# Pooling's window sums as scans on VectorE, and v's weight splits queued earlier, in a transformer-like layer on one core

## The chip, the cores and the metric

The kernel runs on one core of one Trainium2 chip. The metric is the device time of one execution in microseconds (us), as the median of several runs. The engines are named PE (TensorE, matrix products), DVE (VectorE), ACT (ScalarE), POOL (GpSimd) and SP (SyncE, which here only issues DMAs).

## The reference

One layer over 512 tokens of width 1024, all in float32. Cut to what matters here:

```python
POOL_WINDOWS = (2, 4, 8, 16)
def pool_mixer(u, w_pool, pool_scale):
    for g, w in enumerate(POOL_WINDOWS):
        ug = u32[..., g * POOL_GROUP:(g + 1) * POOL_GROUP]
        cs = jnp.cumsum(ug, axis=1)
        cs_lag = jnp.pad(cs, ((0, 0), (w, 0), (0, 0)))[:, :S]
        mean = (cs - cs_lag) / jnp.minimum(pos, float(w))
        outs.append(mean - ug)
    p = jnp.stack(outs, axis=2)
    y = jnp.einsum('bsgi,gij->bsgj', p, w_pool)
    return y.reshape(u.shape) * pool_scale

def reference(x, ...):
    h = rms_norm(x, norm_mix)
    u_pool, u_lru, q, k, v, g_logits = jnp.split(h @ w_in, splits, axis=-1)
    gates = jax.nn.sigmoid(g_logits + b_gate)
    y_pool = pool_mixer(u_pool, w_pool, pool_scale)
    y_lru = rglru_mixer(u_lru, ...)                 # convolution, gates, recurrence over tokens
    y_sb = stick_breaking_attention(rms_norm(q), rms_norm(k), v)
    merged = sum(gates[i] * (y_i @ w_branch[i]))    # three branches
    x = x + merged @ w_out
    h2 = rms_norm(x, norm_ffn)
    return x + (silu(h2 @ w_ffn_gate) * (h2 @ w_ffn_up)) @ w_ffn_down
```

The pooling mixer takes, for each of 4 groups of 256 channels, the mean over the last 2, 4, 8 or 16 tokens, less the token itself.

## The kernel before, in words

Channels lie on the 128 partitions and tokens along the free dimension, so one row of pooling is a tile of 128 channels by 512 tokens; a group `g` has two rows `j`, and a row's names carry both (`p20h` is group 2, row 0). Every product is made of three matmuls (`mm3`, lines 304 to 306): each operand is split into a high part, which ACT copies out, and a low part, which DVE computes as the difference. For a weight tile this is `split_w` (lines 139 and 140, tiles `whi` and `wlo`), for a pooling row `split_hl` (lines 932 and 933, `p20h` and `p20l`), for the attention's weights `wth` and `wtl` (lines 1105 and 1106), for queries and keys `qkh` and `qkl` (lines 1056 and 1057). The next matmuls wait for both.

The order of each engine's instructions is set by a scheduler that goes through the program in the order in which it is written, but takes work of a higher priority sooner: `with tc.high_priority(n)` moves what stands in it ahead by about n places. Weight tiles are made by `emit_next`, three at a time ahead of their use, with a priority of `AHEAD` = 200. Each has one of three buffers, which PE frees.

The program runs in stages. First come the input norm, the gates and the input projection of the recurrence (up to about 139 us). Then v, k and q are projected, each as seven products of half-size blocks by Strassen's scheme: the products are named 11, 12, S2, S1, S3, S4, 22 in this order (v is `t` = 2, its weight splits have keys `("seven", 2, ...)`, and the matmuls stand in line 828). While v is projected, DVE also finishes the recurrence: `lru_input` (704, 705) and `lru_scan` (711, a scan on DVE). S2 adds to the sum in PSUM that ACT copies out of 11 (`snap`, line 841), and S3 to that of S2.

From about 289 us on, the four chunks of pooling are projected (`ps_pool`), in the order 1, 0, 3, 2 of the groups, and then the branch projections (`ps_br`). Between them, from a list of background tasks (`tick`), the attention's heads and the pooling's own steps are put in: ACT copies the row out of PSUM (`evac_u`, line 975, tile `up`); `pool_mean` takes the sums of 2, 4, 8 or 16 tokens by doubling, in one, two, three or four steps of one short copy and one addition each (lines 983 and 984, tiles `pw`), corrects the first columns (987), forms mean less token (989) and splits the result; `pool_back` multiplies with the group's weights (`pps`). In the attention, scores `z` go through two sigmoids (`K`, `A`), a scan on DVE (line 1090, `E`), and a product (1092), are turned on PE (`pw` of line 1103), copied and split (`wth`, `wtl`), and multiplied with v (`py`). The turned tiles, `pq`, `pps` and `py` share three PSUM buffers, so `pq` of one head has to wait until the `wtl` of another has read its tile.

After that come the third branch, the output projection and the feed-forward part, in which nothing changes.

Of the kernel before, what the change touches and what calls it, by code (L numbers as in the profile page):

```python
# [12 lines left out]
ALU = mybir.AluOpType  # L13
# [4 lines left out]
S = 512  # L18
# [15 lines left out]
AHEAD = 200  # L34
# [30 lines left out]
def layer_kernel(ctx: ExitStack, tc: tile.TileContext, x, xt, vecs, w_in, w_qkv7, w_gate7, w_pool, w_rg, w_ig,  # L65
# [3 lines left out]
    dve = nc.vector  # L69
# [216 lines left out]
    def emit_next():  # L286
        i = state["i"]
        if i >= len(specs):
            return
        state["i"] = i + 1  # L290
        key, make = specs[i]
        with tc.high_priority(AHEAD if i > 6 else 0):
            ready[key] = make(str(i))

    def weights(*key):
        while key not in ready:
            emit_next()
        while len(ready) < 3 and state["i"] < state["stop"]:
            emit_next()
        return ready.pop(key)  # L300
# [134 lines left out]
    with ExitStack() as first:  # L435
# [39 lines left out]
        for k in range(2):  # L475
# [4 lines left out]
            make_h(k)  # L480
        load_xt(2)
        emit_next()
        make_h(2)
        load_xt(3)
# [435 lines left out]
    def slot(name, dt=F32, shape=(S,)):  # L920
        return sp.tile([P] + list(shape), dt, tag="s", name=name, bufs=NSP - NLD)
# [7 lines left out]
    def split_hl(src, nm):  # L929
        h = slot_r(nm + "h")  # L930
        l = slot_r(nm + "l")
        act(h, src, AF.Copy)
        dve.tensor_tensor(l, src, h.bitcast(F32), ALU.subtract)
        return h, l

    with ExitStack() as mix:
# [14 lines left out]
        ahead = ap1.tile([P, S], BF16, tag="ahead", name="ahead")  # L951
# [25 lines left out]

        def pool_mean(g, j, u):
            w = 2 << g
            prev, sh = u, 1  # L980
            while sh < w:
                nxt = slot(f"pw{g}{j}{sh}")
                dve.tensor_copy(nxt[:, 0:sh], prev[:, 0:sh])
                dve.tensor_tensor(nxt[:, sh:], prev[:, sh:], prev[:, 0:S - sh], ALU.add)
                prev = nxt
                sh *= 2
            dve.scalar_tensor_tensor(prev[:, 0:w - 1], prev[:, 0:w - 1], float(w),
                                     invpos[:, 0:w - 1], ALU.mult, ALU.mult)
            dve.scalar_tensor_tensor(u, prev, 1.0 / w, u, ALU.mult, ALU.subtract)
            pool_p.setdefault(g, []).append(split_hl(u, f"p{g}{j}"))  # L990
# [21 lines left out]
        def pool_chunk(g):  # L1012
            pss = chan_chunk(("pool", g), hn, 1)
            us = [evac_u(pss[j], f"up{g}{j}", g == POOL[3]) for j in range(2)]
            for j in range(2):
                bg.append(lambda j=j, u=us[j]: pool_mean(g, j, u))
            if g != POOL[0]:
                queue_pool_back(POOL[POOL.index(g) - 1])
# [713 lines left out]
```

## Time and profile before

| | us |
|---|---|
| median of 3 runs | 871.65 (871.23 to 871.83) |
| profiled execution, its own time | 871.86 |
| its span in the trace | 870.1 |
| PE busy | 860.3 |
| DVE busy | 740.7 |
| ACT busy | 522.7 |

The granted clock of PE is full throughout. Busy times are sums over all stages; what an engine costs is seen only in the stretch in which another engine waits for it. In the rows of a timeline the columns are start and duration in us, engine, line, operation, the tile written, the tiles read, and in brackets how long the engine had been idle and what ended that. In a row of who waited for whom they are the waiting engine, its tile and line, what it waited for, and then the total in us, the number of times and the longest.

### The profile page before, as it was taken

The numbers are of one execution on the slowest core, as the hardware profiler recorded it, in microseconds if no ns is written. First come the engines' busy times: TensorE is split into PE (matmuls) and PEld (weight loads), VectorE is DVE, ScalarE is ACT, GpSimd is POOL, SyncE is SP. The second block draws the span as 40 slices with busy tenths as digits, with TensorE's granted clock in tenths as the row PEclk, the third lists the DMA queues.
The fourth block names the chain that finished last, engine by engine and source line by source line (L and its number), as shares of the span: only waits on it lengthen the run. The fifth ranks groups of instructions, "written<-read, shape, count | busy, mean of one in ns | idle before, by whom it ended". The sixth has DMA issues, their size and how long they took to land.

```text
span 870.1 us, 14264 instructions
## 1 busy us (share of the span) xinstructions
PE 860.3 (99%) x5563; PEld 790.2 (91%) x5563; DVE 740.7 (85%) x961; ACT 522.7 (60%) x727; POOL 91.1 (10%) x130
## 2 busy tenths in 40 slices
PE   9999999999999999999999999999999999999998
PEld 7888878888899988889889998889999999999998
DVE  7899897998796598977988796699998888899974
ACT  6554989556966566465664545454555555755642
POOL 1110002232433101000001200000000000121200
PEclk9999999999999999999999999999999999999999
DMA  9586346799592776644636955346543333798913
GB/s 338 164 288 205 98 166 184 212 328 253 174 306 73 236 224 207 217 121 148 212 102 169 197 179 170 97 132 160 147 120 97 108 112 113 230 244 202 191 41 121
DMA packets 116643, 154.08 MB, mean 177 GB/s; under 512 B 8160, under 2 KB 90080, under 8 KB 116576
## 3 DMA queue, kind: packets, MB, share of 16 engines
q1 hardware_dynamic: 103904, 107.30, 38.3%
q0 software_dynamic: 12528, 45.62, 22.0%
q8 instruction: 43, 0.70, 0.3%
q10 hardware_dynamic: 144, 0.26, 0.1%
q14 instruction: 24, 0.20, 0.1%
HBM read 132.71 MB, written 18.87 MB: 174 GB/s over the span
## 4 chain that ended last, share of the span: by engine, by line
PE 84%; DVE 8%; ACT 5%; issue 1%; DMA 1%; SPq 0%; DVEq 0%; ACTq 0%
PE ps_y L313 11%; PE ps_x L313 8%; PE ps_q L828 7%; PE ps_dy L1651 6%; PE ps_dx L1651 5%; PE ps_gate L731 3%; PE ps_bY L1276 2%; PE ps_gy L313 2%; PE ps_br L305 2%; PE ps_br L304 2%; PE ps_br L306 2%; DVE wlo L140 2%; PE ps_bX L1276 2%; PE ps_gx L313 2%; PE ps_lru L304 1%
## 5 line engine op out<-in xcount | busy, mean ns | idle before, releaser
L139 ACT ACTIVATE whi<-raw 128x1024 fp32r<-128x1024 f32 x69 | 72.9, 1056 | 76.1 <-PE ps_out L305 16.0
L140 DVE TENSOR_TENSOR wlo<-raw,whi 128x1024 fp32r<-128x1024 f32 x69 | 84.4, 1224 | 24.7 <-ACT whi L139 24.1
L140 DVE TENSOR_TENSOR wlo<-qw,whi 128x1024 fp32r<-128x1024 f32 x48 | 58.5, 1221 | 16.4 <-ACT whi L139 16.3
L139 ACT ACTIVATE whi<-qw 128x1024 fp32r<-128x1024 f32 x48 | 50.6, 1054 | 28.8 <-PE ps_q L828 14.8
L1437 ACT ACTIVATE wh_S<-w_S 128x1024 fp32r<-128x1024 f32 x36 | 38.3, 1063 | 30.3 <-PE ps_y L313 18.3
L1557 POOL DMA_DIRECT2D dw<-in_w_down_dram x20 | 16.9, 847 | 305.4 <-DMA dw<-in_w_down_dram 261.8
L1438 DVE TENSOR_TENSOR wl_S<-w_S,wh_S 128x1024 fp32r<-128x1024 f32 x36 | 43.9, 1223 | 3.3 <-ACT wh_S L1437 3.3
L1437 ACT ACTIVATE wh<-w 128x1024 fp32r<-128x1024 f32 x27 | 28.6, 1060 | 27.8 <-PE ps_x L313 9.1
L1438 DVE TENSOR_TENSOR wl<-w,wh 128x1024 fp32r<-128x1024 f32 x27 | 33.0, 1223 | 8.2 <-ACT wh L1437 8.2
L1437 ACT ACTIVATE whdS<-dw 128x1024 fp32r<-128x1024 f32 x20 | 21.2, 1060 | 21.6 <-PE ps_dy L1651 10.6
L1438 DVE TENSOR_TENSOR wldS<-dw,whdS 128x1024 fp32r<-128x1024 f32 x20 | 24.3, 1223 | 5.5 <-ACT whdS L1437 5.5
L1090 DVE TENSOR_TENSOR_SCAN E<-K,ahead 128x512 f32<-128x512 f32 (+3 forms) x32 | 25.4, 814 | 4.0 <-ACT K L1086 4.0
L304 PE MATMUL ps_lru<-HH,whi 128*128 128x512 f32 x64 | 24.6, 384 | 0.0
L304 PE MATMUL ps_br<-yph,whi 128*128 128x512 f32 x64 | 24.5, 383 | 0.0
L304 PE MATMUL ps_pool<-HH,whi 128*128 128x512 f32 x64 | 24.5, 383 | 0.0
L304 PE MATMUL ps_br<-yHH,whi 128*128 128x512 f32 x64 | 24.5, 383 | 0.0
L304 PE MATMUL ps_gate<-HH,whi 128*128 128x512 f32 x64 | 24.4, 381 | 0.0
L305 PE MATMUL ps_lru<-HL,whi 128*128 128x512 f32 x64 | 24.3, 379 | 0.0
L306 PE MATMUL ps_lru<-HH,wlo 128*128 128x512 f32 x64 | 24.3, 379 | 0.0
L305 PE MATMUL ps_gate<-HL,whi 128*128 128x512 f32 x64 | 24.3, 379 | 0.0
L306 PE MATMUL ps_gate<-HH,wlo 128*128 128x512 f32 x64 | 24.3, 379 | 0.0
L305 PE MATMUL ps_pool<-HL,whi 128*128 128x512 f32 x64 | 24.3, 379 | 0.0
(740 smaller groups left out, 3445.7 us busy)
## 6 DMA issues: line engine op xcount, KB each, us to landing
raw<-in_w_in_dram SPq DMA_DIRECT2D x31, 512.0 KB, 5.1
qw<-in_w_qkv_dram SPq DMA_DIRECT2D x24, 512.0 KB, 7.1
dw<-in_w_down_dram POOLq DMA_DIRECT2D x20, 512.0 KB, 8.0
w<-in_w_ffn_gate_dram SPq DMA_DIRECT2D x36, 256.0 KB, 3.8
w<-in_w_ffn_up_dram SPq DMA_DIRECT2D x36, 256.0 KB, 4.2
raw<-in_w_branch_dram SPq DMA_DIRECT2D x16, 512.0 KB, 3.6
qw<-in_w_qkv_dram POOLq DMA_DIRECT2D x12, 512.0 KB, 8.0
qd<-r POOLq DMA_DIRECT2D x12, 512.0 KB, 7.3
```

Source lines behind the costliest of these rows:

```text
L139: act(hi, raw, AF.Copy)
L140: dve.tensor_tensor(lo, raw, hi.bitcast(F32), ALU.subtract)
L304: nc.tensor.matmul(ps, lh, rh, start=start, stop=False, skip_group_check=skip)
L305: nc.tensor.matmul(ps, lh, rl, start=False, stop=False, skip_group_check=skip)
L306: nc.tensor.matmul(ps, ll, rh, start=False, stop=stop, skip_group_check=skip)
L313: nc.tensor.matmul(o, a_[a][:, w, k, :], il2(b_[b][:, k, :]), start=first and n == k == 0, stop=last and n == 2 and k == 3, skip_group_che ...
L731: nc.tensor.matmul(pss[n // 2][n % 2], w[:, k % 2, n * P:(n + 1) * P], il(hu[k][x_]), start=k == 0 and w is wh and x_ == 0, stop=k == KT - ...
L828: nc.tensor.matmul(ps[:, a, :], b_[:, k, ts_], il(a_[:, kk, :]), start=first and n == k == 0, stop=n == 2 and k == 3, skip_group_check=True)
L1276: nc.tensor.matmul(o, ah[x_][:, w, k, :], il2(b[k][y_]), start=first_ and n == k == 0, stop=n == 2 and k == 3, skip_group_check=True)
L1437: act(h, src, AF.Copy)
L1438: dve.tensor_tensor(l, src, h.bitcast(F32), ALU.subtract)
L1651: nc.tensor.matmul(o, a_[a][:, w, k0 + k, :], il2(b_[b][:, k, :]), start=first and i == k == 0, stop=last and i == 2 and k == nk - 1, skip ...
```

## The change

Two edits. In `pool_mean` the sum of windows 4, 8 and 16 is made by two scans along the row instead of doublings: the first runs over the first w columns (running sum from 0, with the zeros of the tile `ahead` as second operand), the second over the other 512 - w, adding the new token and subtracting the one that leaves the window, and starting from the first's last column. The window of 2 keeps its copy and addition. In `emit_next` the splits of v's weights get the priority 320 instead of 200.

```diff
-        with tc.high_priority(AHEAD if i > 6 else 0):
+        with tc.high_priority((320 if key[:2] == ("seven", 2) else AHEAD) if i > 6 else 0):
             ready[key] = make(str(i))
...
         def pool_mean(g, j, u):
             w = 2 << g
-            prev, sh = u, 1
-            while sh < w:
-                nxt = slot(f"pw{g}{j}{sh}")
-                dve.tensor_copy(nxt[:, 0:sh], prev[:, 0:sh])
-                dve.tensor_tensor(nxt[:, sh:], prev[:, sh:], prev[:, 0:S - sh], ALU.add)
-                prev = nxt
-                sh *= 2
+            prev = slot(f"pw{g}{j}")
+            if w == 2:
+                dve.tensor_copy(prev[:, 0:1], u[:, 0:1])
+                dve.tensor_tensor(prev[:, 1:], u[:, 1:], u[:, 0:S - 1], ALU.add)
+            else:
+                dve.tensor_tensor_scan(prev[:, 0:w], u[:, 0:w], ahead[:, 0:w], 0.0, ALU.add, ALU.add)
+                dve.tensor_tensor_scan(prev[:, w:], u[:, w:], u[:, 0:S - w], prev[:, w - 1:w], ALU.add, ALU.subtract)
             dve.scalar_tensor_tensor(prev[:, 0:w - 1], prev[:, 0:w - 1], float(w),
                                      invpos[:, 0:w - 1], ALU.mult, ALU.mult)
             dve.scalar_tensor_tensor(u, prev, 1.0 / w, u, ALU.mult, ALU.subtract)
```

On DVE, while v is projected, the order of the splits against the recurrence: `wlo_1395` is of product S2, `wlo_1470` and `wlo_1486` are the first and second split of S3, line 711 is the recurrence's scan.

```order
 L140 TENSOR_TENSOR wlo_1368<-qw_1206,whi_1367 128x1024
 L207 TENSOR_TENSOR qw_1204<-qw_1204,qs_1262 128x1024
+L140 TENSOR_TENSOR wlo_1395<-qs_1262,whi_1394 128x1024
 L207 TENSOR_TENSOR qw_1206<-qw_1206,qs_1302 128x1024
-L140 TENSOR_TENSOR wlo_1395<-qs_1262,whi_1394 128x1024
 L140 TENSOR_TENSOR wlo_1411<-qs_1302,whi_1410 128x1024
```

```order
+L140 TENSOR_TENSOR wlo_1470<-qw_1200,whi_1469 128x1024
 L711 SCALAR_TENSOR_TENSOR li_898<-lt_1118,ls_1249 128x512 x2
-L140 TENSOR_TENSOR wlo_1470<-qw_1200,whi_1469 128x1024
 L711 SCALAR_TENSOR_TENSOR li_1083<-lt_1224,ls_1251 128x512
 L140 TENSOR_TENSOR wlo_1486<-qw_1202,whi_1485 128x1024
```

The first split of S2 passes one addition, the first of S3 passes two scans; the second split of S3 has the same rows ahead of it as before. On ACT, the copies for these splits pass the copy of line 841 that stood ahead of them.

On DVE in the pooling, the sums of the row p20 (numbers of buffers differ between the kernels); a scan is listed as SCALAR_TENSOR_TENSOR with `ahead` or the tile itself as second source. Before:

```order
L983 COPY pw_3444<-up_3347 128x1
L984 TENSOR_TENSOR pw_3444<-up_3347 128x511
L983 COPY pw_3447<-pw_3444 128x2
L984 TENSOR_TENSOR pw_3447<-pw_3444 128x510
L983 COPY pw_3450<-pw_3447 128x4
L984 TENSOR_TENSOR pw_3450<-pw_3447 128x508
L140 TENSOR_TENSOR wlo_3462<-raw_3459,whi_3461 128x1024
L1106 TENSOR_TENSOR wtl_2735<-pw_0_3409,wth_2732 128x512
```

After:

```order
L985 SCALAR_TENSOR_TENSOR pw_3420<-up_3323,ahead 128x8
L986 SCALAR_TENSOR_TENSOR pw_3420<-up_3323,pw_3420 128x504
L987 SCALAR_TENSOR_TENSOR pw_3420<-pw_3420,invpos 128x7
L989 SCALAR_TENSOR_TENSOR up_3323<-pw_3420,up_3323 128x512
L933 TENSOR_TENSOR p20l<-up_3323,p20h 128x512
L140 TENSOR_TENSOR wlo_3432<-raw_3429,whi_3431 128x1024
L1106 TENSOR_TENSOR wtl_2735<-pw_0_3385,wth_2732 128x512
```

Six instructions became two, and the whole rest of the row (987, 989, 933), which stood behind the `wtl` of the attention, now stands ahead of it. On ACT at the same place, before:

```order
L139 ACTIVATE whi_3461<-raw_3459 128x1024
L1105 ACTIVATE wth_2732<-pw_0_3409 128x512
L1105 ACTIVATE wth_2733<-pw_1_3416 128x384
L1105 ACTIVATE wth_2734<-pw_2_3422 128x384
L1086 ACTIVATE K_2741<-z_1_3428,qrs 128x128
```

After:

```order
L932 ACTIVATE p20h<-up_3323 128x512
L139 ACTIVATE whi_3431<-raw_3429 128x1024
L1105 ACTIVATE wth_2732<-pw_0_3385 128x512
L1105 ACTIVATE wth_2733<-pw_1_3392 128x384
L1105 ACTIVATE wth_2734<-pw_2_3398 128x384
```

`p20h`, which waits for DVE's line 989, now stands ahead of `whi` and `wth`; it stood behind them. The row p30 moved in the same way.

## The prediction

> **What bounds the kernel now.** I read the profile's page first, then who made the matrix engine (PE) wait, then the busy time by stretch, then the timelines of PE and the vector engine (DVE) at the places found.
>
> ```profile
> span 870.1 us, 14264 instructions
> PE 860.3 (99%) x5563; PEld 790.2 (91%) x5563; DVE 740.7 (85%) x961; ACT 522.7 (60%) x727; POOL 91.1 (10%) x130
> ```
>
> PE is busy for all but 9.8 us, and the change leaves every matmul where it was. So it can only win back time in which PE stands still, and only where DVE or ACT holds it. The waits of PE, and DVE's load by stretch (columns: window, span, then busy time and count of PE, PEld, DVE, ACT, POOL):
>
> ```profile
> PE pq L1053 <- DVE wtl L1106: 1.7, 2, 1.5
> PE ps_q L828 <- DVE wlo L140: 1.2, 3, 0.7
> PE pps L304 <- DVE qkl L1057: 0.2, 1, 0.2
> ```
>
> ```profile
> 139.00:171.00 32.00, 30.84 (x141) 26.06 (x140) 30.66 (x27) 22.78 (x25) 6.54 (x8) 1.00 0.63 169
> 299.00:350.00 51.00, 51.00 (x266) 45.37 (x265) 46.42 (x84) 32.73 (x58) 4.28 (x8) 1.00 0.76 231
> 350.00:360.00 10.00, 8.49 (x51) 7.38 (x50) 9.93 (x21) 4.09 (x9) 0.00 (x0) 1.00 0.82 273
> 375.00:400.00 25.00, 25.00 (x141) 22.26 (x140) 18.70 (x28) 13.56 (x26) 0.00 (x0) 1.00 0.51 154
> ```
>
> DVE is full at 139 to 171 (v's products beside the recurrence) and at 350 to 360 (pooling beside attention); PE loses 1.2 and 1.5 us there. After 375 DVE has a quarter free, and PE does not wait. Each half of the change touches one of the two. The orders of PE, of the DMA queue of SP and of GpSimd stay as they were, word for word, so no transfer passes another; only DVE and ACT are reordered. The pooling wait in PE's own rows:
>
> ```profile
> 354.62 0.38 PE L306 MATMUL ps_br<-yHH,wlo 128*128 128x512 f32 x1
> 356.51 1.12 PE L1053 MATMUL pq<-idn,at 128*128 128x128 f32 x8 [1.51 <-DVE wtl L1106]
> ...
> 362.09 0.28 PE L306 MATMUL z<-qkh,qkl 128*128 128x256 f32 x1
> 362.54 0.48 PE L304 MATMUL pps<-p30h,wph 128*128 128x512 f32 x1 [0.17 <-DVE qkl L1057]
> 362.86 0.38 PE L305 MATMUL pps<-p30l,wph 128*128 128x512 f32 x1
> ```
>
> Ends of matmuls are modelled, so I count start to start. A 512-column product follows the last after 0.22 us. From 354.62 PE could have gone on at 354.84 but went on at 356.51: 1.67 lost. A 256-column product passes in half that, 0.11: from 362.09 PE could have gone on at 362.20, so 0.34 is lost, and the next step is 0.32 instead of 0.22: 0.10 more, together 0.44. The pooling stretch can give back 1.67 + 0.44 = 2.1 us, whatever DVE saves beyond that.
>
> **The pooling sums.** The new operation is a scan, and the trace has scans of other operands on DVE (busy, mean ns of one):
>
> ```profile
> L989 DVE SCALAR_TENSOR_TENSOR up<-pw,up 128x512 f32<-128x512 f32 x8 | 5.5, 688 | 0.1
> L984 DVE TENSOR_TENSOR pw<-up 128x511 f32<-128x511 f32 x8 | 5.5, 682 | 0.0
> L1090 DVE TENSOR_TENSOR_SCAN E<-K,ahead 128x512 f32<-128x512 f32 x4 | 4.9, 1217 | 0.0
> L1090 DVE TENSOR_TENSOR_SCAN E<-K,ahead 128x128 f32<-128x128 f32 x3 | 1.3, 418 | 0.0
> L987 DVE SCALAR_TENSOR_TENSOR pw<-pw,invpos 128x7 f32<-128x7 f32 x2 | 0.3, 156 | 0.0
> ```
>
> (1217 - 418) / 384 = 2.08 ns a column: a scan of 496 to 508 columns takes 1.18 to 1.21 us, one of 4 to 16 columns 0.16 to 0.19. No row shows a scan of an addition and a subtraction, nor one whose start value is a tensor's column. I take the row's price; from below the bound is a plain addition (0.68), from above twice the row (2.4). [...] At the lower bound the sum below would change by no more than 0.15 us, since PE itself is then the limit.
>
> What the doublings took, and the path to the 1.67 us (DVE):
>
> ```profile
> 328.76 0.14 DVE L983 COPY pw<-up 128x1 f32<-128x1 f32 x1
> 331.80 1.61 DVE L1106 TENSOR_TENSOR wtl<-pw,wth 128x512 fp32r<-128x512 f32 x3
> ...
> 347.01 1.22 DVE L140 TENSOR_TENSOR wlo<-raw,whi 128x1024 fp32r<-128x1024 f32 x1 [0.74 <-ACT whi L139]
> 348.15 0.74 DVE L1003 SCALAR_TENSOR_TENSOR ypl<-pps,vt,yph 128x512 fp32r<-128x512 f32 x1
> 348.81 1.21 DVE L1090 TENSOR_TENSOR_SCAN E<-K,ahead 128x512 f32<-128x512 f32 x1
> ...
> 352.39 0.15 DVE L983 COPY pw<-up 128x1 f32<-128x1 f32 x1
> 354.64 1.22 DVE L140 TENSOR_TENSOR wlo<-raw,whi 128x1024 fp32r<-128x1024 f32 x1
> 355.77 1.62 DVE L1106 TENSOR_TENSOR wtl<-pw,wth 128x512 fp32r<-128x512 f32 x3
> ...
> 361.13 0.69 DVE L933 TENSOR_TENSOR p20l<-up,p20h 128x512 fp32r<-128x512 f32 x1 [0.70 <-ACT p20h L932]
> ```
>
> Four doublings (window 16) took 331.80 - 328.76 = 3.04 us, three (window 8) 354.64 - 352.39 = 2.25: 0.75 a doubling. The two scans take about 0.2 + 1.1 = 1.3 from start to start (an instruction's successor starts some 0.1 before its end: 347.01 to 348.15 for 1.22). So a row of 16 saves 1.7, one of 8 saves 0.95, one of 4 saves 2 x 0.75 - 1.3 = 0.2. Two rows of each: 5.7 us of DVE. Of that, 2 x 0.2 + 2 x 1.7 + 0.95 = 4.8 us lies ahead of 355.77.
>
> PE does not get 4.8, for the order moved as well. The sum's end (`up`) goes to ACT for `p..h` and back for `p..l`; for p11 and p30 the weight split that used to fill that trip now stands behind it, and the price of an empty trip is the 0.70 in the last row above. And on ACT `p20h` now stands ahead of the split and of `wth`, which `wtl` needs. So I walk the path from its last tie to PE: the weight split (`whi`) whose buffer PE frees after this product, and on ACT in the old order
>
> ```profile
> 342.99 0.38 PE L306 MATMUL ps_pool<-HH,wlo 128*128 128x512 f32 x1
> ...
> 350.32 1.06 ACT L139 ACTIVATE whi<-raw 128x1024 fp32r<-128x1024 f32 x1
> 351.28 1.34 ACT L1105 ACTIVATE wth<-pw 128x512 fp32r<-128x512 f32 x3
> ```
>
> In the new order I place that `whi` at 343.45 (one `yph` stands ahead of it on ACT), so its `wlo` on DVE at 344.5, not 347.01. From `wlo` to the pooling of window 8 it took 352.39 - 347.01 = 5.38; one `ypl` (348.81 - 348.15 = 0.66) has moved ahead of it: 4.72, so 349.2. The scans 1.3, the first columns 0.2, the closing product 0.7: 351.4. ACT's `p20h` sends DVE on at 352.1; ACT's `whi` then takes 351.28 - 350.32 = 0.96 and is done at 353.05; DVE's `wlo` 1.13: `wtl` starts at 354.25 instead of 355.77. PE's `pq` started 356.51 - 355.77 = 0.74 after `wtl`: 354.99, against 354.84 at which PE is ready. So 1.52 of the 1.67 comes back. The second wait is for `qkl`, which stood behind the closing product and split of p20; now it follows `wtl` after the three `wtl` (1.5), two scans (1.2), and two passes of 0.6: it starts at 357.55 and is done by 358.3, while PE wants it at 362.20 - 1.52 = 360.7. So the 0.44 goes, with 2 us of cover. Pooling: 1.52 + 0.44 = 1.96 us; bounds 0.9 (one more trip to ACT left open on the path and nothing at the second wait) and 2.1.
>
> **The splits of v's weights.** One DVE order change matters: the first split for S3 passes two scans of the recurrence. DVE, then PE:
>
> ```profile
> 159.05 2.33 DVE L711 TENSOR_TENSOR_SCAN li<-lt,ls 128x512 f32<-128x512 f32 x2
> 161.30 1.20 DVE L140 TENSOR_TENSOR wlo<-qw,whi 128x1024 fp32r<-128x1024 f32 x1
> 162.42 1.22 DVE L711 TENSOR_TENSOR_SCAN li<-lt,ls 128x512 f32<-128x512 f32 x1
> 163.55 1.20 DVE L140 TENSOR_TENSOR wlo<-qw,whi 128x1024 fp32r<-128x1024 f32 x1
> ```
>
> ```profile
> 162.55 0.48 PE L828 MATMUL ps_q<-wlo,hT3h 128*128 128x512 f32 x1 [0.68 <-DVE wlo L140]
> 162.87 0.38 PE L828 MATMUL ps_q<-whi,hT3l 128*128 128x512 f32 x1
> ...
> 165.25 0.38 PE L828 MATMUL ps_q<-wlo,hT3h 128*128 128x512 f32 x1
> ...
> 167.62 0.38 PE L828 MATMUL ps_q2S<-whi,HH 128*128 128x512 f32 x1
> ```
>
> Moved to 159.05, that split ends at 160.25 and PE's wait of 0.68 goes. What is late next is S3's second split: before it stand the same DVE instructions, so it still starts at 163.55 and ends at 163.55 + 1.20 = 164.75. Before, PE came to it at 165.25; now PE is there first and goes on at 164.80, with 0.32 for the first step and ten of 0.216: S4 starts at 167.28 instead of 167.62, a gain of 0.34. The wait that the S2 split removes only brings PE to that same split sooner. On ACT a split passes the copy `r` three times (1.0 us each); PE needs that copy only a product later, so it costs nothing, but 0.3 if it should be late. Bounds: 0 and 1.2 (all three waits).
>
> **Sum.** 1.96 + 0.34 = 2.3 us off the profiled execution's 871.86: 869.56. The median is 0.21 below that execution: **869.4 us**.
>
> **The rivals.** *ACT's order eats the pooling gain.* `p30h` and `p20h` now make ACT wait for DVE ahead of `wth`, `K` and `whi`; one more exposed trip (0.70) and one `whi` (0.96) behind it leave 2.3 - 1.6 = 0.7 us, about 870.9. For it: DVE has 46.42 of 51 us filled before 350 and the path is tight to 0.15 us; against it: 4.8 us saved. [...]
>
> *v gives nothing* because S3's second split falls back by the 0.45 us that it had to spare (164.80 to 165.25): 869.7, still faster.
>
> *Lost again later*: PE, two microseconds sooner, waits for loads that do not come sooner. DMA is 0.51 busy after 375, so I give it little; about 871.
>
> *Slower*: the new scan costs much more than the row. Three large scans lie on the path between 328 and 355; with x more each and nothing hidden, `wtl` comes 3x later. The gains of 1.52 and 0.34 and a 0.2% loss of 1.74 are used up at 3x = 3.6, so from x = 1.2, a scan at twice the row. At 3.0 us (x = 1.8) the time is 871.65 + 5.4 - 1.86 = 875.2. Nothing in the trace speaks for it but that no row shows this form. That the change doesn't do what it says I exclude: the order shows both scans and the moved splits.
>
> **Chances.** Forecast 0.54, v nothing 0.10 (both faster); ACT's order 0.20 and lost later 0.07 (both within); slower 0.09. A measurement tells about 0.2%, 1.74 us, so faster means below 869.9: 0.64; within 0.27; slower 0.09. The range runs from 868.4 (2.1 and 1.2 us together) to 871.2, past the two cases within; it leaves out the slow scan and the edges.
>
> **What would show it.** Right: large scans of about 1.2 us; PE's wait for `wtl` near 355 under 0.3 us and for `qkl` near 360 gone; one wait of PE for the second S3 split near 164, S4 about 0.3 us earlier; no new wait near 334. Wrong: scans over 2 us, PE held by `wtl` at 334, or the gain gone by 460.

## The result, and the profile after

| | us |
|---|---|
| median before, 22 runs beside those of the change | 871.62 (870.99 to 872.79) |
| median after, 22 runs | 870.28 (869.95 to 871.04) |
| ratio, 95% interval | 0.9986 (0.998 to 0.9992) |
| profiled execution of after, its own time | 870.05 |
| its span | 868.3 |

The change is faster by 1.3 us. That is inside the forecast range, 0.9 us above the forecast, and at 0.14% it lies within the 0.2%, for which I had given 0.27. The head of the page of after (engine, busy us, share of the span, instructions), then who made PE wait:

```profile
span 868.3 us, 14234 instructions
PE 859.3 (99%) x5563; PEld 789.9 (91%) x5563; DVE 736.4 (85%) x937; ACT 522.3 (60%) x727; POOL 91.0 (10%) x130
```

```profile
PE ps_q L828 <- DVE wlo L140: 1.1, 2, 0.8
PE pq L1053 <- DVE wtl L1106: 1.0, 3, 0.7
```

The row of `pps` that waited for `qkl` is gone, but `pq` still waits 1.0 us for `wtl`, in three places instead of two. PE's timeline after, at four places (`...` marks rows left out, here and below):

```profile
164.04 0.48 PE L828 MATMUL ps_q<-wlo,hT3h 128*128 128x512 f32 x1 [0.84 <-DVE wlo L140]
...
332.38 0.38 PE L306 MATMUL ps_pool<-HH,wlo 128*128 128x512 f32 x1
332.94 0.80 PE L1053 MATMUL pq<-idn,at 128*128 128x128 f32 x5 [0.18 <-DVE wtl L1106]
...
354.23 0.38 PE L306 MATMUL ps_br<-yHH,wlo 128*128 128x512 f32 x1
355.26 0.79 PE L1053 MATMUL pq<-idn,at 128*128 128x128 f32 x5 [0.66 <-DVE wtl L1106]
...
360.84 0.28 PE L306 MATMUL z<-qkh,qkl 128*128 128x256 f32 x1
360.95 0.38 PE L304 MATMUL pps<-p30h,wph 128*128 128x512 f32 x1
```

Start to start, less the 0.22 us of a product: at 355 PE loses 0.81 where it lost 1.67, and at 333 it now loses 0.34. At 361 the products follow without a gap. In v two waits are left: 0.84 us for the second split of S3, and 0.24 us at 144.80, which the trace of before has as well (0.25 at 145.56).

To see where the span's 1.8 us went, I count in each trace from one matmul's start to another's, because the start of the first product of v wanders: it came at 139.75 us in the trace of before, at 139.00 after, and between 138.98 and 141.51 in the runs below, though nothing ahead of it differs. Those 0.75 us are not the change's. The rest: 0.35 us between v's first product and S4 (27.87 to 27.52), 0.57 between the first pooling product and the first `pps` of p20 (82.31 to 81.74), 0.1 behind it. Together 1.0; the medians differ by 1.3 with an interval of 0.7 to 1.7 by the ratio.

### The profile page after: what moved, and what is told of

It reads as the page before. It is cut to its first block, busy times and chain, and to the rows that moved or that the text cites. A ratio compares the mean times of both kernels' runs of the same rounds, so it can differ in the third digit from the quotient of the medians.

```text
span 868.3 us, 14234 instructions
## 1 busy us (share of the span) xinstructions
PE 859.3 (99%) x5563; PEld 789.9 (91%) x5563; DVE 736.4 (85%) x937; ACT 522.3 (60%) x727; POOL 91.0 (10%) x130
## 4 chain that ended last, share of the span: by engine, by line
PE 56%; DVE 5%; ACT 2%; issue 1%; DMA 1%; SPq 0%; DVEq 0%; ACTq 0%
PE ps_y L313 11%; PE ps_x L313 8%; PE ps_dy L1651 6%; PE ps_dx L1651 5%; PE ps_bY L1276 2%; PE ps_br L305 2%; PE ps_br L304 2%; PE ps_br L306 2%; PE ps_bX L1276 2%; PE ps_out L304 1%; PE ps_out L305 1%; PE ps_out L306 1%; DVE wlo L140 1%; PE ps_fu L306 1%; PE ps_fu L304 1%; PE ps_fu L305 1%
## 5 line engine op out<-in xcount | busy, mean ns | idle before, releaser
L305 PE MATMUL ps_br<-yHL,whi 128*128 128x512 f32 x64 | 24.4, 381 | 0.0
L306 PE MATMUL ps_pool<-HH,wlo 128*128 128x512 f32 x64 | 24.3, 379 | 0.0
L305 PE MATMUL ps_br<-ypl,whi 128*128 128x512 f32 x64 | 24.3, 379 | 0.0
```

Of the source, the lines that this page charges most:

```text
L305: nc.tensor.matmul(ps, lh, rl, start=False, stop=False, skip_group_check=skip)
L306: nc.tensor.matmul(ps, ll, rh, start=False, stop=stop, skip_group_check=skip)
```

## The experiments

All times in this table come from the starts of the same matmuls and splits in each kernel's trace. "v" runs from the first `ps_q` to S4, "pooling" from the first `ps_pool` product to the first `pps` of p20; the second `wtl` and the `pq` that waits for it are counted from that first pooling product. The last two columns are the change against before of the whole way from the first `ps_q` to the first `ps_bY` product of the third branch, and that of the medians against the runs of before on the same chip.

| kernel | v | wtl | pq | pooling | stretches | medians |
|---|---|---|---|---|---|---|
| before | 27.87 | 67.02 | 67.76 | 82.31 | | |
| after | 27.52 | 66.89 | 67.63 | 81.74 | -1.03 | -1.34 |
| e1 v alone | 27.51 | 67.03 | 67.77 | 82.30 | -0.39 | -0.11 |
| e2 scans alone | 27.86 | 66.89 | 67.63 | 81.74 | -0.70 | -0.90 |
| e3 scans, both parts by DVE | 27.52 | 64.98 | 66.29 | 80.32 | -2.46 | -2.14 |
| e4 S3's scan held back | 26.41 | 66.89 | 67.63 | 81.74 | -1.00 | -0.95 |
| e5 scans, low part later | 27.52 | 66.55 | 67.50 | 81.52 | -1.25 | -1.24 |
| e6 doublings, low part later | 27.52 | 68.05 | 68.80 | 84.04 | +1.28 | +1.58 |
| e7 other forms of the scan | 27.51 | 66.49 | 67.23 | 81.33 | -1.44 | -1.01 (one time) |
| e8 scans, whole split later | 27.51 | 64.39 | 66.55 | 80.58 | -2.21 | -2.21 |
| e9 doublings, both parts by DVE | 27.52 | 66.96 | 67.70 | 82.04 | -0.72 | -0.78 |

The stretches give each median to within 0.5 us, so the rest of the program hands on what PE wins here. Kernels with the same pooling order agree in it to 0.01 us (after, e2, e4), wherever their start lay.

**e1, the splits of v alone.** The kernel before with one line:

```diff
-        with tc.high_priority(AHEAD if i > 6 else 0):
+        with tc.high_priority((320 if key[:2] == ("seven", 2) else AHEAD) if i > 6 else 0):
```

> Only the splits of v's weights are queued earlier; pooling keeps its doublings. The stretches are measured on PE between marks that every kernel has: from v's first product (q0) to the start of S4, from there to the first product of pooling, from there to the product with p20, and to the end. Before: 27.87, 121.13, 82.31. Theory A (S3's second split binds): q0 to S4 27.53, one PE wait for a split near S3 of 0.8 us in place of 0.68, the other stretches as before, time 0.3 to 0.4 us under before. Rival (the split order does nothing, the profile's gain is all a luckier start): 27.87 and no difference in time.

Measured 871.36 us, ratio 0.9995 (0.9986 to 1.0005): the time alone can't tell it from no change. The trace can: S4 comes 0.36 us sooner, and what is left is the wait that the prediction named, for S3's second split:

```profile
164.12 0.48 PE L828 MATMUL ps_q<-wlo,hT3h 128*128 128x512 f32 x1 [0.84 <-DVE wlo L140]
```

**e2, the scans alone.** The changed kernel with `AHEAD` for every split again, the reverse of e1's line.

> Only the scans; v's splits at their old priority. Theory A (the scans take work off DVE, but the row's high part now waits on ACT ahead of the attention's copies, so the path to wtl hardly shortens): pooling to the product with p20 81.7 to 81.9 against 82.31, with waits of PE for wtl at two places (about 0.2 and 0.7), time 0.4 to 0.7 us under before. Rival (the v half makes PE come early and so creates the wait; alone the scans give their full 1.9): 80.4 and 1.9 us under before.

Measured 870.57 us, ratio 0.9988 (0.9979 to 0.9996). The pooling stretch is that of after, v that of before. The two halves don't touch each other.

**e3, both parts of a row by DVE.** This takes ACT out of the row's way: the high part is a cast on DVE.

```diff
-            pool_p.setdefault(g, []).append(split_hl(u, f"p{g}{j}"))
+            h, l = slot_r(f"p{g}{j}h"), slot_r(f"p{g}{j}l")
+            dve.tensor_copy(h, u)
+            dve.tensor_tensor(l, u, h.bitcast(F32), ALU.subtract)
+            pool_p.setdefault(g, []).append((h, l))
```

> The changed kernel, but the high part of every pooling row is made by DVE (a cast of 128x512) and not by ACT, so that no trip to ACT stands between the closing product and the low part. The same values, and 8 casts more on DVE (a cast of this size took 0.42 in the first stage; from start to start about 0.35), 8 copies fewer on ACT. Theory A (the trips and what waits behind them on ACT hold the path): DVE's idle time between the first scan and the second wtl falls from 5.3 to under 3.5 us, wtl starts 1 us or more earlier against PE, PE's waits for wtl near 333 and 355 fall under 0.2 together, pooling to p20's product 80.5 to 80.9 against 81.74, time 0.7 to 1.2 us under the changed kernel. Rival (DVE's load itself is the bound, scans at 1.25 instead of 1.18): 7 casts more ahead of wtl make it 2.4 us later, PE waits 2 to 3 us near 355, time 1 to 2 us over the changed kernel.

Measured 869.33 us, ratio 0.9973 (0.9964 to 0.9982). PE's timeline first; then the stretch from the first pooling sum to the second `wtl` in before, in after and in e3 (window, its length, then busy time and count of PE, PEld, DVE, ACT, POOL):

```profile
353.92 0.38 PE L306 MATMUL ps_br<-yHH,wlo 128*128 128x512 f32 x1
354.13 0.93 PE L1056 MATMUL pq<-idn,at 128*128 128x128 f32 x7
```

```profile
303.49:355.77 52.28, 51.51 (x270) 45.61 (x268) 48.96 (x91) 33.11 (x60) 4.28 (x8) 1.00 0.75 234
```

```profile
302.52:354.52 52.00, 51.79 (x269) 45.35 (x267) 46.71 (x74) 31.71 (x58) 4.28 (x8) 1.00 0.76 235
```

```profile
302.58:352.82 50.24, 50.24 (x265) 44.69 (x263) 49.03 (x81) 29.93 (x54) 4.28 (x8) 1.00 0.76 235
```

PE passes the place at 355 without a wait. The scans had taken 2.25 us of work off DVE (48.96 to 46.71), net of the close of row p20, which moved into the stretch. But the stretch became only 0.28 us shorter, as DVE stood idle for 5.29 us in it instead of 3.32: after has four empty trips to `p..h` there (0.76 us three times and 0.69), before had one (0.76). With the casts DVE has more to do than after and is through 1.8 us sooner, since it hardly waits. So here DVE, the busier of the two, took work back from ACT and won: its 46.71 us of work became 49.03, and its 5.29 us of idle time 1.21. The step cost 2.32 us of work and took away 4.08 us of waiting.

**e4, the recurrence's scans of chunk 3 kept in the order in which they are written**, to see what stands behind S3's wait:

```diff
-                dve.tensor_tensor_scan(h[:, j, :], t[:, j, :], s_[:, j, :], 0.0, ALU.mult, ALU.add)
+                s = dve.tensor_tensor_scan(h[:, j, :], t[:, j, :], s_[:, j, :], 0.0, ALU.mult, ALU.add)
+                if c == 3:
+                    tc.keep_in_program_order(s)
```

> The changed kernel, with the recurrence's last two scans (chunk 3) held behind the splits that are queued at that point, so that the second split of S3 passes them. Theory A (that split was late only for the three scans ahead of it): it ends about 1.1 us earlier, PE's wait of 0.84 near S3 goes, q0 to S4 26.4 to 26.7 against 27.52; time 0.8 to 1.1 us under the changed kernel. Rival (its high part on ACT, which waits for PE to free a buffer, binds next): the wait shrinks to 0.3 to 0.6 only and the time by 0.3 to 0.5; or the scans come back as a wait for k's splits and nothing is gained.

Measured 870.52 us, ratio 0.9986 (0.9977 to 0.9995), the gain of the change and no more. S4 came 1.1 us sooner than after, and PE lost it again later, most of it in product S2 of k, by a wait for a split that the scans now delay (DVE has no gap between the moved scans and that split; PE's timeline):

```profile
187.80 0.48 PE L830 MATMUL ps_q<-wlo,hT2h 128*128 128x512 f32 x1 [0.62 <-DVE wlo L140]
```

From S4 to the first pooling product it took 122.25 us where all others take 121.1. So moving the scans moved the wait: with DVE this full, it goes where the scans go. The 0.8 to 1.1 us that the first theory gave did not come; the last case of the rival, a wait for k's splits, did.

**e5, only the low part later.** e3 left open which side of the trip costs: DVE standing before `p..l` for ACT's answer, or ACT standing before `p..h` for DVE's sum. Here `p..l` of a row is written at the start of the next row:

```diff
+        def flush_lows():
+            while lows:
+                l, u, h = lows.pop()
+                dve.tensor_tensor(l, u, h.bitcast(F32), ALU.subtract)
         def pool_mean(g, j, u):
+            flush_lows()
...
-            pool_p.setdefault(g, []).append(split_hl(u, f"p{g}{j}"))
+            h, l = slot_r(f"p{g}{j}h"), slot_r(f"p{g}{j}l")
+            act(h, u, AF.Copy)
+            pool_p.setdefault(g, []).append((h, l))
+            lows.append((l, u, h))
```

> The changed kernel, with one thing moved: the low part of a pooling row (p..l on DVE) is written not right behind its sum but at the start of the next row, so that DVE doesn't stand behind ACT's p..h. Every operation is kept, PE's order too. First theory (the gain of the scans was eaten by DVE's empty trips to ACT: p11l, p30l, p31l 0.76 each, p20l 0.69, and by the weight split that follows them): those waits of DVE are gone, wtl of the second pooling step starts at least 1 us sooner against the first pooling product, pq at 66.2 to 66.7 us after that product (67.63 in the changed kernel), the time is 869.2 to 869.6. Rival (ACT, which stands before p..h until the sum is done, holds the weight split, so DVE's place for p..l is of no account): pq stays at 67.4 to 67.6, the time at 870.1 to 870.4.

Measured 870.13 us, ratio 0.9981 (0.9973 to 0.999): the first theory fell. The waits for `p..h` ahead of the second `wtl` are gone, but DVE waits for other work of ACT instead (DVE, then ACT):

```profile
313.02 1.23 DVE L140 TENSOR_TENSOR wlo<-raw,whi 128x1024 fp32r<-128x1024 f32 x1 [1.71 <-ACT whi L139]
...
343.40 0.69 DVE L1103 TENSOR_TENSOR_SCAN E<-K,ahead 128x256 f32<-128x256 f32 x1 [1.61 <-ACT K L1099]
```

```profile
311.41 0.63 ACT L999 ACTIVATE p11h<-up 128x512 fp32r<-128x512 f32 x1 [4.18 <-DVE up L997]
311.94 1.04 ACT L139 ACTIVATE whi<-raw 128x1024 fp32r<-128x1024 f32 x1
...
341.89 0.63 ACT L999 ACTIVATE p31h<-up 128x512 fp32r<-128x512 f32 x1 [3.81 <-DVE up L997]
342.43 0.58 ACT L1131 ACTIVATE ysb<-py 128x512 f32<-128x512 f32 x1
342.90 0.47 ACT L1099 ACTIVATE K<-z,qrs 128x256 f32<-128x256 f32 x1
```

ACT has stood idle for 4.18 and 3.81 us before `p..h`, until DVE's sum was done. `whi` and `K`, which have nothing to do with the row, stand behind `p..h` in ACT's order and start only after it, and DVE, done with the row, waits for just these. The `K` of 342.90 could have gone sooner: PE had begun the last product of its `z` 3.6 us before (PE's timeline).

```profile
339.31 0.28 PE L306 MATMUL z<-qkh,qkl 128*128 128x256 f32 x1
```

**e6, the same move with doublings**: before with e1's line and e5's edit.

> The kernel before with the two edits that are no scans: v's splits at the greater advance, and the low part of a pooling row at the start of the next row, sums still by doublings. It tells what the scans are worth once the trips are covered. First theory (trips and doublings both load the path to wtl; the exposed trip of p31l was 0.76, and the last doubling of window 8, 0.75, now stands behind wtl): some 1.2 to 1.5 of the 1.67 us at pq come back, the second wait stays, the time is 869.8 to 870.3, so above the scans with the same move by 0.4 to 0.8. Rival (DVE is filled by the doublings, so only the scans can bring pq forward): pq at 67.5 or later after the first pooling product, the time 871.0 to 871.5.

Measured 872.95 us, ratio 1.0018 (1.0009 to 1.0026): slower than before. The time lies outside what either theory gave; `pq`, at 68.80, is where the rival had it (67.5 or later). PE's waits and one row of DVE:

```profile
PE pq L1066 <- DVE wtl L1119: 1.8, 2, 1.6
...
PE pps L304 <- DVE qkl L1070: 0.9, 1, 0.9
```

```profile
348.20 0.69 DVE L1077 TENSOR_TENSOR vl<-at,vh 128x512 fp32r<-128x512 f32 x1 [1.76 <-ACT vh L1076]
```

As in e5, DVE runs into ACT's queue: `vh` stands there behind `p31h`, and the row's last step (`up`), which `p31h` needs, starts 55.6 us after the first pooling product, in e5 53.0.

**e7, other forms of the large scan**, to see why it takes more than forecast.

```diff
-                dve.tensor_tensor_scan(prev[:, w:], u[:, w:], u[:, 0:S - w], prev[:, w - 1:w], ALU.add, ALU.subtract)
+                if w == 16:
+                    dve.tensor_tensor_scan(prev[:, w:], u[:, w:], u[:, 0:S - w], 0.0, ALU.add, ALU.subtract)
+                elif w == 8:
+                    dve.tensor_tensor_scan(prev[:, w:], u[:, w:], ahead[:, 0:S - w], prev[:, w - 1:w], ALU.add, ALU.subtract)
+                else:
+                    dve.tensor_tensor_scan(prev[:, w:], ahead[:, 0:S - w], u[:, w:], prev[:, w - 1:w], ALU.mult, ALU.add)
```

> The changed kernel with three forms of the large pooling scan, to see what its 1.25 to 1.27 us (1.18 to 1.21 forecast) is made of: window 16 starts from the constant 0 instead of a column, window 8 has the constant row as its second operand in place of the shifted u, window 4 multiplies and adds from a column. The pooled sums are other numbers than before. If the start column costs the 0.07, window 16 falls to 1.18 and 8 and 4 stay at 1.26 and 1.27; if the unaligned second operand does, window 8 falls to 1.19 and the others stay; if the pair add and subtract does, window 4 falls to 1.20. If it is none, all three stay. The time is within 0.3 us of the changed kernel's.

The sums of this kernel are not the pooling's: the window of 16 starts from 0, that of 8 does not take out the tokens that leave it, and that of 4 multiplies with the constant row. One time, 870.36 us. The scans in groups (busy, mean ns of one), first of after, then of e7:

```profile
L986 DVE TENSOR_TENSOR_SCAN pw<-up,pw 128x508 f32<-128x508 f32 x2 | 2.5, 1274 | 0.0
L986 DVE TENSOR_TENSOR_SCAN pw<-up,pw 128x504 f32<-128x504 f32 x2 | 2.5, 1258 | 0.0
L986 DVE TENSOR_TENSOR_SCAN pw<-up,pw 128x496 f32<-128x496 f32 x2 | 2.5, 1251 | 0.1
```

```profile
L991 DVE TENSOR_TENSOR_SCAN pw<-ahead,pw,up 128x508 f32<-128x508 bf16 x2 | 2.5, 1274 | 0.1
L989 DVE TENSOR_TENSOR_SCAN pw<-up,pw,ahead 128x504 f32<-128x504 f32 x2 | 2.5, 1256 | 0.0
L987 DVE TENSOR_TENSOR_SCAN pw<-up 128x496 f32<-128x496 f32 x2 | 2.3, 1170 | 0.0
```

Only the window of 16 fell, by 0.08 us (1251 to 1170 ns): it is the start from a column. Multiply and add, with the constant row as an operand, took what add and subtract take in after (1274 and 1274 ns for 508 columns), and the constant row in place of the shifted `u` what the shifted `u` takes (1256 and 1258 ns for 504).

**e8, the whole split later**: as e5, but `p..h` on ACT goes to the start of the next row too, so that ACT does not stand before the unfinished sum of `p31` any more (no idle time before `p31h`, where after has 3.33 us). No operation is added or taken out, and PE's order is that of after; on SP one weight load changes places with the small load behind it.

```diff
+        def split_late():
+            while todo:
+                l, u, h = todo.pop()
+                act(h, u, AF.Copy)
+                dve.tensor_tensor(l, u, h.bitcast(F32), ALU.subtract)
         def pool_mean(g, j, u):
+            split_late()
...
+            pool_p.setdefault(g, []).append((h, l))
+            todo.append((l, u, h))
```

> The changed kernel with the whole split of a pooling row moved to the start of the next row: not only p..l on DVE, as in the run before, but p..h on ACT too, so that ACT no longer stands in front of a sum that is not done while whi, K and wth queue up behind p..h. No operation is taken out, PE's order is kept. ACT theory (what eats the gain is ACT standing in p..h until DVE's sum ends: when only p..l was moved, DVE's waits moved to wlo behind whi, 1.71, and to E behind K, 1.61): those waits go, wtl of the second pooling step starts 65.0 to 66.0 us after the first pooling product (66.89 in the changed kernel, 64.98 with DVE making both parts), pq at 66.2 to 66.7, the time is 869.0 to 869.6. Rival (with DVE making both parts it was the trip as a whole, and any round through ACT costs the same wherever it stands): wtl at 66.4 to 66.9, the time 869.9 to 870.3.

Measured 869.27 us, ratio 0.9977 (0.9967 to 0.9986), by the medians the same gain as e3, with all of the split's work on the engines where it was. The second `wtl` comes 2.5 us sooner than after, and 0.6 sooner than I had given for it. On ACT, `whi` now waits for PE to free its buffer:

```profile
342.44 1.06 ACT L139 ACTIVATE whi<-raw 128x1024 fp32r<-128x1024 f32 x1 [1.58 <-PE ps_pool L305]
...
349.56 1.06 ACT L139 ACTIVATE whi<-raw 128x1024 fp32r<-128x1024 f32 x1 [2.29 <-PE ps_br L305]
```

PE starts `pq` 2.16 us after `wtl`, so it is no longer held there; what it loses at that place is a wait for a load (PE's timeline), for which the pooling stretch is 0.26 us longer than e3's:

```profile
353.36 0.48 PE L305 MATMUL ps_br<-yHL,whi 128*128 128x512 f32 x1 [0.19 <-DMA yHL<-ydl]
```

**e9, doublings with both parts by DVE**: e3 without its scans, which gives the fourth corner of a square (doublings or scans, the high part by ACT or by DVE).

> The kernel before with v's splits at the greater advance and both parts of a pooling row made by DVE, sums by doublings: the run with DVE making both parts, less the scans. It tells what the scans are worth where no trip to ACT hides them. Theory (without the trips DVE is full from the first pooling sum to wtl, 49.0 busy of 50.2 us, so each microsecond of DVE counts): the doublings put back 2 x 0.2 + 2 x 1.65 + 0.9 = 4.6 us ahead of the second wtl, which starts at 69.0 to 69.8 us after the first pooling product (64.98 with scans), pq at 69.8 to 70.6, the time is 873.2 to 874.3. Rival (the trips alone were the cost, the doublings ran in time that DVE had over): wtl at 65 to 66.5, the time 869.3 to 870.5.

Measured 870.7 us, ratio 0.9994 (0.9985 to 1.0003), and `wtl` at 66.96: between what the two theories gave, nearer to the rival. The stretch to the second `wtl`, and DVE behind that `wtl`:

```profile
302.66:354.88 52.22, 51.78 (x270) 45.67 (x268) 50.96 (x97) 30.19 (x54) 4.28 (x8) 1.00 0.76 233
```

```profile
354.88 1.61 DVE L1109 TENSOR_TENSOR wtl<-pw,wth 128x512 fp32r<-128x512 f32 x3
...
358.85 0.69 DVE L989 SCALAR_TENSOR_TENSOR up<-pw,up 128x512 f32<-128x512 f32 x1
```

DVE works 50.96 of 52.22 us where e3 works 49.03 of 50.24: each microsecond that the scans save is one that `wtl` comes sooner (1.93 and 1.98). So between these two runs DVE's load is what counts, as the theory has it; its 4.6 us was too much by 2.6, for I had left out that with doublings the close of row p20 (its `up` at 358.85) stands behind `wtl`, as in the kernel before, and with scans ahead of it. In e3 that close takes 1.97 us, from 349.71 to 351.68 (DVE):

```profile
349.71 0.14 DVE L987 SCALAR_TENSOR_TENSOR pw<-pw,invpos 128x7 f32<-128x7 f32 x1
349.89 0.69 DVE L989 SCALAR_TENSOR_TENSOR up<-pw,up 128x512 f32<-128x512 f32 x1
350.61 0.43 DVE L991 CAST p20h<-up 128x512 fp32r<-128x512 f32 x1
...
351.68 1.22 DVE L140 TENSOR_TENSOR wlo<-raw,whi 128x1024 fp32r<-128x1024 f32 x1
```

The square, second `wtl` after the first pooling product: doublings 67.02 with ACT's high part and 66.96 without, scans 66.89 and 64.98. Either step alone gives 0.1 us, both give 2.0. The step to DVE has its own price: against before, e9's casts add 2.00 us of work to DVE (48.96 to 50.96) and take 2.06 of idle time away (3.32 to 1.26), so alone it is worth nothing. And this is `wtl`'s square. In the pooling stretch the single steps give 0.27 and 0.57 and both together 1.99; the medians, each good to some 0.8 us, give 0.7, 1.2 and 2.0 against e1 and can't tell this from a plain sum.

## Why the prediction was right or wrong, step by step

The measured time lies inside the range because the range had been drawn past a rival; the way to the forecast itself was wrong for pooling, which gave 0.57 us where I had 1.96. So the number held by the width of the range and not by its reason. Two of the signs set down came out against me: PE's wait near 355 is 0.66 us and not under 0.3, and there is a new wait for `wtl` near 333.

**What PE can win** was right. The most that any run took out of the pooling stretch was 1.99 us (e3), against 2.1 written down, and nothing was won past it.

**The price of the scan** was near: 1.25 to 1.27 us for 1.18 to 1.21. The pair of scans took 1.39 from start to start (DVE, after) and not 1.3; with a constant as start it took 1.19 (e7):

```profile
328.58 0.18 DVE L985 TENSOR_TENSOR_SCAN pw<-up,ahead 128x16 f32<-128x16 f32 x1
328.80 1.25 DVE L986 TENSOR_TENSOR_SCAN pw<-up,pw 128x496 f32<-128x496 f32 x1
329.97 0.15 DVE L987 SCALAR_TENSOR_TENSOR pw<-pw,invpos 128x15 f32<-128x15 f32 x1
...
331.60 0.69 DVE L933 TENSOR_TENSOR p30l<-up,p30h 128x512 fp32r<-128x512 f32 x1 [0.76 <-ACT p30h L932]
```

```profile
329.14 0.18 DVE L985 TENSOR_TENSOR_SCAN pw<-up,ahead 128x16 f32<-128x16 f32 x1
329.24 1.17 DVE L987 TENSOR_TENSOR_SCAN pw<-up 128x496 f32<-128x496 f32 x1
330.33 0.15 DVE L992 SCALAR_TENSOR_TENSOR pw<-pw,invpos 128x15 f32<-128x15 f32 x1
```

**The walk "from its last tie to PE"** is the step that failed. I took `whi` to be tied to PE's product at 342.99 and placed it at 343.45, with one `yph` ahead of it on ACT; that is 54.70 us after the first pooling product. ACT after:

```profile
340.63 0.63 ACT L932 ACTIVATE p31h<-up 128x512 fp32r<-128x512 f32 x1 [3.33 <-DVE up L989]
341.16 0.58 ACT L1118 ACTIVATE ysb<-py 128x512 f32<-128x512 f32 x1
...
343.44 1.07 ACT L139 ACTIVATE whi<-raw 128x1024 fp32r<-128x1024 f32 x1
...
351.77 0.63 ACT L932 ACTIVATE p20h<-up 128x512 fp32r<-128x512 f32 x1 [4.00 <-DVE up L989]
352.31 1.04 ACT L139 ACTIVATE whi<-raw 128x1024 fp32r<-128x1024 f32 x1
```

It started at 343.44, which is 55.81 us after the first pooling product of this trace (287.63). It did not wait for PE: it stood without a gap in the row behind `p31h`, and `p31h` had waited 3.33 us for DVE's sum. So the tie was to DVE, by way of ACT's order, and from the `wlo` at 305.12 us on, whose `whi` had waited for PE, the path was one chain of DVE and ACT in which no wait for PE counts. That made `whi` 1.11 us later than the walk has it. The trace of before has the same tie (ACT), which the walk leaves out:

```profile
343.91 0.63 ACT L932 ACTIVATE p31h<-up 128x512 fp32r<-128x512 f32 x1 [3.55 <-DVE up L989]
...
345.93 1.05 ACT L139 ACTIVATE whi<-raw 128x1024 fp32r<-128x1024 f32 x1
```

Counted from the first pooling product, the scans brought `p31h` 2.16 us forward (55.16 to 53.00). Of that, `whi` kept 1.37, since `K`, `A` and a `yph` now stand between them, and `wtl` 0.13, since the close of row p20 now lies between `whi` and `wtl`.

Against the walk: from `whi` to `wtl` I had 10.80 us and it took 11.08, the scans' 0.1 among them: 0.28 more. With the 1.11 of `whi` that is 1.39, the forecast 1.96 less the measured 0.57.

Where `whi` does wait for PE, in e8, it starts 54.45 us after the first pooling product, so without that chain the tie is the one I took. `wtl` then comes at 64.39 in e8 and at 64.98 in e3, sooner than the walk's 65.50 (354.25 less 288.75). That `pq` of e3 starts at 66.29, where the walk has 66.24 (354.99 less 288.75), does not confirm the walk: PE's own row is the limit there, not `wtl`.

The new wait at 333, which I had ruled out, is of the same kind: `p30l` stands behind an empty trip of 0.76 ahead of `wtl`. Three of the prediction's sums are also slightly off by their own terms: 353.05 + 1.13 is 354.18 and not 354.25, `qkl` would start at 358.15 and not 357.55, and the lower bound for pooling is 0.8 and not 0.9. None of them moves the forecast by more than 0.1 us.

**The second wait**, 0.44, went as predicted.

**The rival "ACT's order eats the pooling gain"** is what happened, in kind: that ACT, waiting for DVE, holds up `whi` and `K` is what e5 and e8 show. Its price of 1.6 us came to 1.39, but not by the rows that it named: the 1.11 came by `p31h`, which stood ahead of `whi` before the change too, and the trip for `p20h` was in the walk already. That the two figures are so near is in part luck. It left 0.7 us of gain; the stretches show 1.03 and the medians 1.34, and which of these two is nearer stays open, since the interval of the ratio holds both.

**v** was right in place and size: 0.34 forecast, 0.35 measured, and what is late next is S3's second split. *v gives nothing*, *lost again later* and *slower* fell: from `ps_bY` to the end the two traces take 398.42 and 398.43 us.

## What to carry to other kernels

Before pricing a faster operation by its own engine's load, look up which engine takes its result, and what stands in that engine's order behind the instruction that waits. Here, of 2.25 us of work saved on DVE, 0.28 was left: first DVE stood in empty trips to ACT, and when these were covered (e5), it stood for `whi` (1.71 us) and `K` (1.61), which ACT had behind a row that DVE was still summing. When a saving and a wait lie on the same chain, the saving alone can show little (0.1 us in `wtl`) where the two together give 2.0 or more (e3, e8), so a fusion that disappoints is worth a second run with the consumer moved out of the way. And a walk along a path is only as good as its anchor: read in the trace what released the instruction it starts from, and count from a mark that moves with it.

## What the runs showed of the hardware that I had not expected

In the row p30 the pair of scans whose second starts from a column that the first has just written took 1.39 us from start to start (after), and 1.19 where the second starts from a constant (e7). Of these 0.20 us, 0.08 is the large scan's own duration (1251 and 1170 ns for 496 columns), the rest its later start (0.22 and 0.10 us after the small scan's). Whether the column as such costs this, or its having just been written, no run tells apart. A cast of 128x512 to the matmul's type took 0.43 us on DVE (`p20h` in e3) where the same copy took 0.63 on ACT (`p20h` in after).
